# Dense expert tiles moved from the middle of the token order to its end in a streaming-encoder layer

## The chip, the core and the metric

The kernel runs on one core of one Trainium2 chip. The metric is the device time of one execution in microseconds. The core has TensorE (PE, matrix products), VectorE (DVE, elementwise work and reductions), ScalarE (ACT), GpSimd (POOL) and SyncE (SP); each takes its instructions strictly in the order in which the program lists them. SP and POOL issue DMA transfers between DRAM and the on-chip memory.

## The reference

One layer for two request groups that share weights, 1024 prompt tokens and 64 sample tokens of width 1024. Its first half is a sum of three gated branches (an mLSTM, a spatial gating unit, a cross attention). Its second half, which the change is about, is a retrieval over 16384 experts:

```python
q = (xb @ w_pq).reshape(PEER_BLOCK, PEER_HEADS, PEER_DQ)
s1 = jnp.einsum('thd,kd->thk', q[..., :half], k_sub1)
s2 = jnp.einsum('thd,kd->thk', q[..., half:], k_sub2)
v1, i1 = lax.top_k(s1, PEER_TOPK)
v2, i2 = lax.top_k(s2, PEER_TOPK)
cand = v1[..., :, None] + v2[..., None, :]            # 16 x 16 sums
sc, pos = lax.top_k(cand, PEER_TOPK)
e = jnp.take_along_axis(cidx, pos, axis=-1)           # 8 heads x 16 experts a token
g = jax.nn.softmax(sc, axis=-1)
a = jax.nn.gelu(jnp.einsum('tkd,td->tk', u_exp[e], xb))
out = jnp.einsum('tk,tkd->td', g * a, v_exp[e])
```

So each token picks 128 of the 16384 experts (8 heads, 16 each), takes a dot product with a row of `u_exp` for each, and sums rows of `v_exp` with the weights that come out. Outputs are the two normalised results and the states and caches of the first half.

## The kernel before

**Tiles and blocks.** The tokens stand in nine tiles: 0 to 7 of 128 prompt tokens and "s" of 64 sample tokens. `BLOCKS` groups them: [0, 1], [2, 3, 4, "s"], [5, 6, 7]. The first phase runs block after block: `main_block` does the projections and the output projection on PE, `mlstm` and `side` the branches, and `retrieve` the scores against the sub-keys and, on DVE, the first top-16 of each head. `choose_tile` then does, once for each tile and almost wholly on DVE, the second top-16 over 54 candidate sums, the decoding of the expert numbers and the softmax. In the second phase PE works through all 16384 experts for the dense tiles.

**Two ways through the experts.** Tiles in `GT` gather: for each of a token's 128 experts a row of `u_exp` is fetched by an indirect DMA that POOL issues (L1018, one for 128 rows of 4 KB; the sample tile packs two picks of 64 tokens into one), and DVE takes the dot product (L1031, here called a u) into a column of `av`; later a row of `v_exp` is fetched the same way and DVE adds it, weighted, to the tile's sum (L1039, a v). With four tiles of 128 and the one of 64 this is 576 u and 576 v. The landing buffers are three for u (`BU`) and four for v (`BV`), seven for the last tile's v; a buffer comes free when its u or v has run on DVE. The u of a tile run beside the v of the tile before it.

Tiles in `DENSE` (512 tokens) are instead multiplied with all experts on PE: `hidden` computes 256 experts for 512 tokens and applies the gelu, `times_g` multiplies by a table of weights that is zero but for the chosen experts, `weigh` splits the result in a high and a low part, and `dense` multiplies by `v_exp` (L1258 to L1260). The operands are split in high and low parts, which costs three products each; the low part of every weight piece is taken on DVE (L280, `wl`).

**The table.** `dense` builds it before its own expert loop, tile by tile in the order of `CHOOSE`, in groups of four tokens: DVE writes 0/1 rows by comparing with the two key numbers (L1187) and multiplies one of them by the softmax weights (L1191), here together called the hots, 256 instructions; PE multiplies the two (L1200), ACT copies the result to `sg`, and SP stores it to `gd` in DRAM. It needs `d{t}`, the end of `choose_tile` of that tile. Only four pieces of `hidden` can run ahead of the table; the expert loop on PE starts when the whole table is in DRAM and its first part has been loaded back (`g<-gd`).

**What sets the order.** Each part is a generator; `Flow.run` takes the one that has got least far, by the numbers that the generators yield, or passes over one that waits for a signal. A list scheduler then orders each engine's instructions further when the program is built. `experts` yields 2.5 a gather in the first phase and 2.2 in the second; the hots yield 1.2 a group of four tokens. In the last block `choose_tile` of the gathering tiles 6 and 7 waits for the signal "weights", which `dense` gives after its last hots.

Of the kernel before, what the change touches and what calls it, by code (L numbers as in the profile page):

```python
# [7 lines left out]
F32 = mybir.dt.float32  # L8
F32R = mybir.dt.float32r
BF = mybir.dt.bfloat16  # L10
I32 = mybir.dt.int32
# [54 lines left out]
def tile_stream_step(ctx: ExitStack, tc: tile.TileContext, a: dict, out: dict):  # L66
    nc = tc.nc
    V, S, T, G, SP = nc.vector, nc.scalar, nc.tensor, nc.gpsimd, nc.sync


    BLOCKS = [[0, 1], [2, 3, 4, "s"], [5, 6, 7]]
    TILES = [t for b in BLOCKS for t in b]

    DENSE = [2, 3, 4, 5]
    NT = max(len(b) for b in BLOCKS)
    ND = len(DENSE)
    ROWS_OF = {t: 64 if t == "s" else 128 for t in TILES}
    TD = 128 * ND
# [5 lines left out]
    gp = pool("gp", 1)  # L84
    kp = pool("kp", 1)
# [9 lines left out]
    now = {"dp": None}  # L95
# [238 lines left out]
    fl = Flow()  # L334
    st = {}
# [504 lines left out]
    def choose_tile(b, t):  # L840

        L = ROWS_OF[t]
        v16, i16 = st["k", t]
        scv = kp.tile([128, 8, 16], F32, name="scv", bufs=1)[0:L]
        if b == len(BLOCKS) - 1 and t not in DENSE:

            yield "weights"
            V.tensor_copy(scv[0:1, 0, 0:1], st["weights"][0:1])
        pos = kp.tile([128, 8, 16], U32, name="pos", bufs=1)[0:L]
        ib = kp.tile([128, 256], BF, name="ib", bufs=1)[0:L].rearrange("p (a k) -> p a k", k=16)  # L850
        V.tensor_copy(ib.rearrange("p (s h) k -> p s h k", s=2), i16.rearrange("p (h s) k -> p s h k", s=2))
# [45 lines left out]
                    V.tensor_tensor(ef, ef, oh[:, 0], op=ALU.add)  # L897
                yield 1.7
        if t not in DENSE:
            if GT.index(t) >= 3:  # L900
                yield f"free{GT[GT.index(t) - 3]}"
            go = gp.tile([128, 128], F32, name="gg", bufs=3)
            e = gp.tile([128, 128], I32, name="e", bufs=3)

            for q in range(128 // L):
                V.scalar_tensor_tensor(e[q * L:q * L + L, 0:L], ef[:, q * 64:q * 64 + L], 128.0,
                                       ef[:, 128 + q * 64:128 + q * 64 + L], op0=ALU.mult, op1=ALU.add)
        gg = kp.tile([128, 8, 16], F32, name="ggd")[0:L]
# [19 lines left out]


    GT = [t for t in TILES if t not in DENSE]  # L930
    CHOOSE = [t for b in BLOCKS for t in sorted(b, key=lambda t: (t in DENSE) != (b is BLOCKS[-1]))]

    def out_rows(t, x, r, gfin):
        n = ROWS_OF[t]
# [4 lines left out]
    def experts():  # L939
# [14 lines left out]
        def end_u(t):  # L954
            _, av = st_u.pop(t)
            e, gg = st.pop(("e", t))
            L = ROWS_OF[t]
            av, gg = av[:, 0:L], gg[:, 0:L]
            t1 = gp.tile([128, 128], F32, name="w2", bufs=2)[:, 0:L]
            S.activation(t1, av, AF.Square, scale=GELU_C ** 0.5)  # L960
            V.scalar_tensor_tensor(t1, t1, 1.0, av, op0=ALU.add, op1=ALU.mult)
            S.activation(t1, t1, AF.Tanh, scale=GELU_S)
            V.scalar_tensor_tensor(t1, t1, 1.0, av, op0=ALU.add, op1=ALU.mult)
            V.scalar_tensor_tensor(t1, t1, 0.5, gg, op0=ALU.mult, op1=ALU.mult)
            st_v[t] = (e, t1)
            fl.signal(f"u{t}")
# [82 lines left out]
        for s_ in range(len(ops)):  # L1049
            while nxt < len(ops) and (nxt <= s_ or can_issue(ops[nxt])):  # L1050
                kind, t, j = ops[nxt]
                ready = f"e{t}"
                if kind == "u" and ready not in fl.done:
                    if nxt > s_:
                        break
                    yield ready
                issue(ops[nxt])
                nxt += 1
            consume(ops[s_])

            yield 2.5 if now["dp"] is None else 2.2

    phase1 = [main(), mlstm(), side(), retrieve()]
    for g in phase1:
# [9 lines left out]
    dp = pool("dp", 1)  # L1074
# [65 lines left out]
    def dense():  # L1140
# [16 lines left out]
        x = hp.tile([128, 2560], BF, name="hotx")  # L1157
        hots.append((x[:, 0:1024], x[:, 1024:2560]))
        hots = [[x.rearrange("p (j c t) -> p j c t", c=128, t=4) for x in h] for h in hots]
        nd1 = 0  # L1160
        for i, t in sorted(enumerate(DENSE), key=lambda x: CHOOSE.index(x[1])):
            n = ROWS_OF[t]
            yield f"d{t}"
            k_ = kp.tile([128, 3, 128], F32, name="dk", tag="k4", bufs=3)[0:n]
            SP.dma_start(k_, dkd[t])
            cs = slice(i * 128, i * 128 + n)
            p = two_banks()[:, 0, :]
            for j in range(3):
                T.transpose(p[:, j * 128:j * 128 + n], k_[:, j, :], ident[0:n, 0:n])
            S.copy(kb[:, :, cs], p.rearrange("p (s t) -> p s t", s=4)[:, 0:2, 0:n])  # L1170
            gf = kp.tile([128, 128], F32, name="gf", tag="k4", bufs=3)
            S.copy(gb[:, 0, cs], p[:, 256:256 + n])
            V.tensor_tensor(gf[:, 0:n], p[:, 256:256 + n], gb[:, 0, cs], op=ALU.subtract)
            S.copy(gb[:, 1, cs], gf[:, 0:n])
            V.tensor_tensor(gb[:, 2, cs], gf[:, 0:n], gb[:, 1, cs], op=ALU.subtract)
            V.tensor_copy(gf_[:, cs], gb[:, 2, cs])
            yield 3.0

            for t0 in range(i * 128, i * 128 + n, 32):
                sg = hp.tile([128, 32, 4, 32], F32, name="sg", bufs=2)  # L1180
                for t1 in range(0, 32, 8):
                    p = two_banks()
                    for b in range(2):
                        tb = t0 + t1 + 4 * b
                        ts = slice(tb, tb + 4)
                        eq, pr = hots[tb // 4 % len(hots)]
                        V.tensor_tensor(eq, io[:, None].to_broadcast([128, 2, 128, 4]),  # L1187
                                        kb[:, :, None, ts].to_broadcast([128, 2, 128, 4]), op=ALU.is_equal)

                        nd = 2 + b  # L1190
                        V.tensor_tensor(pr[:, 0:nd], eq[:, 0, None].to_broadcast([128, nd, 128, 4]),  # L1191
                                        gb[:, 0:nd, None, ts].to_broadcast([128, nd, 128, 4]), op=ALU.mult)
                        for j in range(nd, 3):
                            for t2 in range(4):
                                S.activation(pr[:, j, :, t2], eq[:, 0, :, t2], AF.Copy,
                                             scale=gf_[:, tb + t2:tb + t2 + 1])

                        for t2 in range(4):
                            for j in range(3):
                                T.matmul(p[:, b, t2 * 128:(t2 + 1) * 128], eq[:, 1, :, t2], pr[:, j, :, t2],  # L1200
                                         start=(j == 0), stop=(j == 2))
                        yield 1.2
                    S.copy(sg[:, :, :, t1:t1 + 8].rearrange("p g c t -> p (g c) t"),
                           p.rearrange("p b (t e) -> p e (b t)", t=4))
                    yield 0.4
                nd1 += 32
                if nd1 == TD:
                    st["weights"] = tok = kp.tile([128, 1], F32, name="tok")
                    V.tensor_copy(tok, sg[:, 0, 0, 0:1])
                    fl.signal("weights")  # L1210
                SP.dma_start(gd[:, :, t0 // 32].rearrange("g p c t -> p g (c t)"),
                             sg.rearrange("p g c t -> p g (c t)"))
        yield "ahead"
# [149 lines left out]
```

## Time and profile before

| | |
|---|---|
| median of 3 runs | 3675.89 us (3674.61 to 3696.73) |
| the profiled execution | 3700.63 us, its span 3698.9 us |
| PE busy | 3280.4 us, 89% |
| DVE busy | 3102.7 us, 84% |
| POOL busy | 1721.0 us, 47% |
| ACT busy | 1367.2 us, 37% |
| moved by DMA | 1024.78 MB, mean 277 GB/s |
| mean granted PE clock | 0.932 of full speed |

The engines work at the same time, so their shares don't add to 100%. Shares over the whole span hide that different stretches have different limits. The first phase ends on DVE at about 1912 us (the first `dxl`, L1133, the operand of the dense tiles); the hots run from 1925 to 2242 us; from 2290 us to the end PE does the dense expert loop.

### The profile page before, as it was taken

Reading aid. Unit: us, or ns where it says so; the run is one execution under the profiler, and the core shown is the slowest. Engines: PE = TensorE matmul, PEld = TensorE weight load, DVE = VectorE, ACT = ScalarE, POOL = GpSimd, SP = SyncE. Lnnn points to the kernel's source line nnn. Section 1 sums busy time; section 2 is a strip of 40 time slices with the busy share of each in tenths; the row PEclk is TensorE's granted clock in tenths of the full one; section 3 lists DMA queues with packets and bytes.
Section 4 is the critical chain, followed back from the end, with each engine's and each line's share of the span. In section 5 each row is a group of like instructions: output and inputs, shape, how many; then the busy total and the mean of one; then the engine's idle time right before and its main releaser. Section 6 shows DMA issues by size and latency. Waiting matters only on the chain.

```text
span 3698.9 us, 46231 instructions
## 1 busy us (share of the span) xinstructions
PE 3280.4 (89%) x15364; PEld 2632.8 (71%) x15364; DVE 3102.7 (84%) x6492; ACT 1367.2 (37%) x2479; POOL 1721.0 (47%) x1208
## 2 busy tenths in 40 slices
PE   8999998889996595898939765998999999999998
PEld 7787876576675473776938664876678888888886
DVE  5556797768899999899998999887798888879984
ACT  5555533423333242333415653322233333333332
POOL 1001334447765775465333475444465555446540
PEclk9999999999998697998959767999999999999999
DMA  7556477788897887898867788888899999989982
GB/s 230 148 165 188 152 245 248 254 279 321 320 367 273 272 306 252 276 334 285 302 209 220 235 269 292 312 287 276 295 376 337 337 339 337 328 282 386 356 303 85
DMA packets 447436, 1024.78 MB, mean 277 GB/s; under 512 B 32182, under 2 KB 169566, under 8 KB 443100
## 3 DMA queue, kind: packets, MB, share of 16 engines
q0 software_dynamic: 166528, 604.58, 47.0%
q1 hardware_dynamic: 276828, 413.06, 33.6%
q10 hardware_dynamic: 3840, 4.20, 0.3%
q8 instruction: 120, 1.97, 0.2%
q14 instruction: 120, 0.98, 0.1%
HBM read 968.44 MB, written 53.26 MB: 276 GB/s over the span
## 4 chain that ended last, share of the span: by engine, by line
PE 46%; DVE 20%; issue 13%; DMA 11%; POOL 8%; ACT 1%; POOLq 0%; DVEq 0%; ACTq 0%; SPq 0%
DMA gu<-in_u_exp_dram,e 7%; POOL gu L1018 5%; PE po L1260 5%; PE po L1259 5%; PE po L1258 5%; PE ph L1109 4%; PE ph L1111 4%; PE ph L1110 4%; DVE gacc L1039 4%; DVE gu L1031 4%; PE acc L312 3%; PE acc L311 3%; PE acc L313 3%; DVE wl L280 2%; DMA gv<-in_v_exp_dram,e 2%
## 5 line engine op out<-in xcount | busy, mean ns | idle before, releaser
L1018 POOL DMA_INDIRECT gv<-in_v_exp_dram,e x522 | 842.1, 1613 | 671.9 <-DVE gacc L1039 294.9
L1018 POOL DMA_INDIRECT gu<-in_u_exp_dram,e x576 | 756.8, 1314 | 774.6 <-DVE gu L1031 491.2
L277 ACT CAST wh<-wraw 128x512 fp32r<-128x512 f32 x994 | 613.0, 622 | 1347.9 <-PE ph L1110 481.5
L1031 DVE SCALAR_TENSOR_TENSOR gu<-gu,gx 128x1024 f32<-128x1024 f32 x576 | 701.6, 1220 | 195.2 <-DMA gu<-in_u_exp_dram,e 192.7
L280 DVE TENSOR_TENSOR wl<-wraw,wh 128x512 fp32r<-128x512 f32 x962 | 655.0, 686 | 228.4 <-ACT wh L277 226.2
L1039 DVE SCALAR_TENSOR_TENSOR gacc<-gv,w,gacc 128x1024 f32<-128x1024 f32 x448 | 573.1, 1279 | 33.3 <-DMA gv<-in_v_exp_dram,e 32.8
L312 PE MATMUL acc<-wl,half 128*128 128x512 f32 (+1 forms) x1152 | 474.1, 412 | 4.1 <-DVE wl L280 4.1
L313 PE MATMUL acc<-wh,half 128*128 128x512 f32 (+1 forms) x1152 | 456.2, 402 | 0.0
L1258 PE MATMUL po<-wh,W 128*128 128x512 f32 x1024 | 403.2, 399 | 32.6 <-ACT W L1228 32.6
L1111 PE MATMUL ph<-dxh,wl 128*128 128x512 f32 x1024 | 403.0, 394 | 18.5 <-DVE wl L280 18.4
L311 PE MATMUL acc<-wh,half 128*128 128x512 f32 (+1 forms) x1152 | 412.0, 410 | 6.5 <-ACT uB L470 5.1
L1259 PE MATMUL po<-wl,W 128*128 128x512 f32 x1024 | 408.7, 399 | 7.9 <-DVE wl L280 7.8
L1260 PE MATMUL po<-wh,W 128*128 128x512 f32 x1024 | 407.6, 398 | 0.6 <-DVE W L1229 0.6
L1109 PE MATMUL ph<-dxh,wh 128*128 128x512 f32 x1024 | 401.5, 392 | 1.3 <-DVE dxl L1133 1.3
L1110 PE MATMUL ph<-dxl,wh 128*128 128x512 f32 x1024 | 400.9, 391 | 0.0
L328 PE MATMUL acc<-half,wh 128*128 128x256 f32 (+2 forms) x768 | 250.2, 346 | 17.8 <-ACT wh L277 13.1
L311 PEld LDWEIGHTS acc<-wh,half 128*128 128x128 f32 (+1 forms) x1152 | 210.3, 184 | 77.8 <-issue 15.1
L312 PEld LDWEIGHTS acc<-wl,half 128*128 128x128 f32 (+1 forms) x1152 | 211.7, 184 | 71.4 <-issue 12.5
L329 PE MATMUL acc<-half,wh 128*128 128x256 f32 (+2 forms) x768 | 258.9, 342 | 0.0
L1258 PEld LDWEIGHTS po<-wh,W 128*128 128x128 f32 x1024 | 194.0, 189 | 80.3 <-issue 33.7
L313 PEld LDWEIGHTS acc<-wh,half 128*128 128x128 f32 (+1 forms) x1152 | 210.7, 184 | 54.4 <-issue 1.9
L330 PE MATMUL acc<-half,wl 128*128 128x256 f32 (+2 forms) x768 | 228.4, 343 | 15.5 <-DVE wl L280 8.5
(446 smaller groups left out, 5062.1 us busy)
## 6 DMA issues: line engine op xcount, KB each, us to landing
wraw<-in_w_in_dram SPq DMA_DIRECT2D x216, 512.0 KB
wraw<-in_v_exp_dram SPq DMA_DIRECT2D x126, 512.0 KB
wraw<-in_u_exp_t_dram SPq DMA_DIRECT2D x67, 512.0 KB
gd<-sg SPq DMA_DIRECT2D x16, 2048.0 KB
g<-gd SPq DMA_DIRECT2D x32, 1024.0 KB
wrawx<-in_u_exp_t_dram SPq DMA_DIRECT2D x61, 512.0 KB
wraw<-in_w_pq_dram SPq DMA_DIRECT2D x48, 512.0 KB
wraw<-in_w_out_dram SPq DMA_DIRECT2D x24, 512.0 KB
```

What stands on the lines that cost most here:

```text
L277: S.copy(h, t)
L280: E.tensor_tensor(l, t, h.bitcast(F32), op=ALU.subtract)
L311: T.matmul(ps[i], xh[:, cs], h, start=(k == 0), stop=False)
L312: T.matmul(ps[i], xh[:, cs], l, start=False, stop=False)
L313: T.matmul(ps[i], xl[:, cs], h, start=False, stop=(last and b is None))
L1018: G.indirect_dma_start(out=tl, out_offset=None, in_=src, in_offset=bass.IndirectOffsetOnAxis(ap=col, axis=0))
L1031: V.scalar_tensor_tensor(tl, tl, 1.0, xn, op0=ALU.mult, op1=ALU.mult, accum_out=av[:, j:j + 1])
L1039: V.scalar_tensor_tensor(x2, gt_.pop(op), st_v[t][1][:, j:j + 1], x2, op0=ALU.mult, op1=ALU.add)
L1111: T.matmul(o, l[:, cs], xh[:, k + kk, :], start=False, stop=(k + kk == KD - 1))
L1258: T.matmul(o, hi, h, start=(q == 0 and k == 0), stop=False)
L1259: T.matmul(o, hi, l, start=False, stop=False)
L1260: T.matmul(o, lo, h, start=False, stop=(q == GP - 1 and k == 1))
```

## The change

Six things: `DENSE` becomes [4, 5, 6, 7], so that tiles 0, 1, 2, 3 and "s" gather (all in the first two blocks) and three of the four dense tiles are in the last block; the wait for "weights", with the token that gave it, goes; `CHOOSE` takes gathering tiles first in every block, the last one too; the buffers of the gathering tiles' expert numbers and weights become four of each instead of three, and `w2` one instead of two; `experts` yields 3.0 in the first phase and 2.0 in the second (2.5 and 2.2); the hots yield 0.3 instead of 1.2.

```diff
--- before.py
+++ after.py
@@ -71,7 +71,7 @@
     BLOCKS = [[0, 1], [2, 3, 4, "s"], [5, 6, 7]]
     TILES = [t for b in BLOCKS for t in b]
 
-    DENSE = [2, 3, 4, 5]
+    DENSE = [4, 5, 6, 7]
     NT = max(len(b) for b in BLOCKS)
     ND = len(DENSE)
     ROWS_OF = {t: 64 if t == "s" else 128 for t in TILES}
@@ -842,10 +842,6 @@
         L = ROWS_OF[t]
         v16, i16 = st["k", t]
         scv = kp.tile([128, 8, 16], F32, name="scv", bufs=1)[0:L]
-        if b == len(BLOCKS) - 1 and t not in DENSE:
-
-            yield "weights"
-            V.tensor_copy(scv[0:1, 0, 0:1], st["weights"][0:1])
         pos = kp.tile([128, 8, 16], U32, name="pos", bufs=1)[0:L]
         ib = kp.tile([128, 256], BF, name="ib", bufs=1)[0:L].rearrange("p (a k) -> p a k", k=16)
         V.tensor_copy(ib.rearrange("p (s h) k -> p s h k", s=2), i16.rearrange("p (h s) k -> p s h k", s=2))
@@ -897,10 +893,10 @@
                     V.tensor_tensor(ef, ef, oh[:, 0], op=ALU.add)
                 yield 1.7
         if t not in DENSE:
-            if GT.index(t) >= 3:
-                yield f"free{GT[GT.index(t) - 3]}"
-            go = gp.tile([128, 128], F32, name="gg", bufs=3)
-            e = gp.tile([128, 128], I32, name="e", bufs=3)
+            if GT.index(t) >= 4:
+                yield f"free{GT[GT.index(t) - 4]}"
+            go = gp.tile([128, 128], F32, name="gg", bufs=4)
+            e = gp.tile([128, 128], I32, name="e", bufs=4)
 
             for q in range(128 // L):
                 V.scalar_tensor_tensor(e[q * L:q * L + L, 0:L], ef[:, q * 64:q * 64 + L], 128.0,
@@ -928,7 +924,7 @@
 
 
     GT = [t for t in TILES if t not in DENSE]
-    CHOOSE = [t for b in BLOCKS for t in sorted(b, key=lambda t: (t in DENSE) != (b is BLOCKS[-1]))]
+    CHOOSE = [t for b in BLOCKS for t in sorted(b, key=lambda t: t in DENSE)]
 
     def out_rows(t, x, r, gfin):
         n = ROWS_OF[t]
@@ -956,7 +952,7 @@
             e, gg = st.pop(("e", t))
             L = ROWS_OF[t]
             av, gg = av[:, 0:L], gg[:, 0:L]
-            t1 = gp.tile([128, 128], F32, name="w2", bufs=2)[:, 0:L]
+            t1 = gp.tile([128, 128], F32, name="w2", bufs=1)[:, 0:L]
             S.activation(t1, av, AF.Square, scale=GELU_C ** 0.5)
             V.scalar_tensor_tensor(t1, t1, 1.0, av, op0=ALU.add, op1=ALU.mult)
             S.activation(t1, t1, AF.Tanh, scale=GELU_S)
@@ -1058,7 +1054,7 @@
                 nxt += 1
             consume(ops[s_])
 
-            yield 2.5 if now["dp"] is None else 2.2
+            yield 3.0 if now["dp"] is None else 2.0
 
     phase1 = [main(), mlstm(), side(), retrieve()]
     for g in phase1:
@@ -1157,7 +1153,6 @@
         x = hp.tile([128, 2560], BF, name="hotx")
         hots.append((x[:, 0:1024], x[:, 1024:2560]))
         hots = [[x.rearrange("p (j c t) -> p j c t", c=128, t=4) for x in h] for h in hots]
-        nd1 = 0
         for i, t in sorted(enumerate(DENSE), key=lambda x: CHOOSE.index(x[1])):
             n = ROWS_OF[t]
             yield f"d{t}"
@@ -1199,15 +1194,10 @@
                             for j in range(3):
                                 T.matmul(p[:, b, t2 * 128:(t2 + 1) * 128], eq[:, 1, :, t2], pr[:, j, :, t2],
                                          start=(j == 0), stop=(j == 2))
-                        yield 1.2
+                        yield 0.3
                     S.copy(sg[:, :, :, t1:t1 + 8].rearrange("p g c t -> p (g c) t"),
                            p.rearrange("p b (t e) -> p e (b t)", t=4))
                     yield 0.4
-                nd1 += 32
-                if nd1 == TD:
-                    st["weights"] = tok = kp.tile([128, 1], F32, name="tok")
-                    V.tensor_copy(tok, sg[:, 0, 0, 0:1])
-                    fl.signal("weights")
                 SP.dma_start(gd[:, :, t0 // 32].rearrange("g p c t -> p g (c t)"),
                              sg.rearrange("p g c t -> p g (c t)"))
         yield "ahead"
```

On DVE, near the end of the first phase (around the 560th of the 1088 `wl`; L1039 before and L1035 after are the v, L1027 is the u after), before the change:

```order
L1039 SCALAR_TENSOR_TENSOR gacc<-gv,w_17058,gacc 128x1024
L280 TENSOR_TENSOR wl<-wraw,wh 128x512
L892 TENSOR_TENSOR oh<-oh 128x512
L194 TENSOR_TENSOR rn<-rn 128x3
L280 TENSOR_TENSOR wl<-wraw,wh 128x512
L1039 SCALAR_TENSOR_TENSOR gacc<-gv,w_17058,gacc 128x1024
L896 TENSOR_TENSOR oh<-oh 128x256
L889 SCALAR_TENSOR_TENSOR oh<-xy,ib 128x256 x2
```

and of the change, at the same place:

```order
L1027 SCALAR_TENSOR_TENSOR gu,av<-gu,gx 128x1024
L1035 SCALAR_TENSOR_TENSOR gacc<-gv,w_16080,gacc 128x1024
L195 TENSOR_TENSOR rn<-rn 128x3
L280 TENSOR_TENSOR wl<-wraw,wh 128x512 x2
L1035 SCALAR_TENSOR_TENSOR gacc<-gv,w_16080,gacc 128x1024
L197 SCALAR_TENSOR_TENSOR rn<-rn 128x3
L1027 SCALAR_TENSOR_TENSOR gu,av<-gu,gx 128x1024 x2
```

Before, no u is left there, since the next gathering tile (6) is not chosen yet; after, u of tile 2 or 3 stand there beside the v, and the choosing of a dense tile (`oh`) has moved back.

On DVE, in the middle of the hots (L1187 and L1191 before, L1182 and L1186 after; `hot`, `one` and `hotx` are their rows, `oh` and `ei` belong to `choose_tile`), before the change:

```order
L1191 TENSOR_TENSOR one<-one 128x1536
L1191 TENSOR_TENSOR hotx<-hotx,one 128x1536
L1039 SCALAR_TENSOR_TENSOR gacc<-gv,w_21390,gacc 128x1024
L1187 TENSOR_TENSOR hot<-one 128x1024
L1039 SCALAR_TENSOR_TENSOR gacc<-gv,w_21390,gacc 128x1024
L1187 TENSOR_TENSOR one<-one 128x1024
L1191 TENSOR_TENSOR hot<-hot,one 128x1024
L1187 TENSOR_TENSOR one<-one 128x1024
L1039 SCALAR_TENSOR_TENSOR gacc<-gv,w_21390,gacc 128x1024
L1187 TENSOR_TENSOR hotx<-one 128x1024
L1191 TENSOR_TENSOR one<-one 128x1536
```

and of the change, during the choosing of tile 7:

```order
L1186 TENSOR_TENSOR hot<-hot,one 128x1024
L1186 TENSOR_TENSOR one<-one 128x1536
L1027 SCALAR_TENSOR_TENSOR gu,av<-gu,gx 128x1024
L1035 SCALAR_TENSOR_TENSOR gacc<-gv,w_22386,gacc 128x1024
L1186 TENSOR_TENSOR one<-one 128x1024
L1186 TENSOR_TENSOR hotx<-hotx,one 128x1536
L885 SCALAR_TENSOR_TENSOR oh<-xy,ib 128x256 x2
L1182 TENSOR_TENSOR hot<-one 128x1024
L1027 SCALAR_TENSOR_TENSOR gu,av<-gu,gx 128x1024
L1182 TENSOR_TENSOR one<-one 128x1024
L1035 SCALAR_TENSOR_TENSOR gacc<-gv,w_22386,gacc 128x1024
```

Before, only v of tiles 1 and "s" stand between the hots; after, u and v both, and the instructions that choose a later dense tile. Counted over the whole order: from the first `dxl` to the last of the 256 hots there stand 74 v and no u before, 122 v and 174 u after; the choosing there is 115 instructions before and 363 after.

On DVE, in the dense loop at the 660th of the 1088 `wl` (L1093 and L1089 are `times_g`, L1229 and L1219 `weigh`), before the change:

```order
L1031 SCALAR_TENSOR_TENSOR gu,av<-gu,gx 128x1024
L280 TENSOR_TENSOR wl<-wraw,wh 128x512
L1093 TENSOR_TENSOR ge<-ge,g_20380 128x1024
L1031 SCALAR_TENSOR_TENSOR gu,av<-gu,gx 128x1024 x2
L280 TENSOR_TENSOR wl<-wrawx,wh 128x512
L1229 TENSOR_TENSOR W<-ge,W 128x1024
L1031 SCALAR_TENSOR_TENSOR gu,av<-gu,gx 128x1024
```

and of the change:

```order
L1035 SCALAR_TENSOR_TENSOR gacc<-gv,w_26527,gacc 128x1024
L280 TENSOR_TENSOR wl<-wraw,wh 128x512
L1089 TENSOR_TENSOR ge<-ge,g_20015 128x1024
L1035 SCALAR_TENSOR_TENSOR gacc<-gv,w_26527,gacc 128x1024
L280 TENSOR_TENSOR wl<-wrawx,wh 128x512
L1035 SCALAR_TENSOR_TENSOR gacc<-gv,w_26527,gacc 128x1024 x2
L1219 TENSOR_TENSOR W<-ge,W 128x1024
```

Behind the last hots there are 256 u and 275 v before and 6 u and 237 v after; the last v stands at the 1061st `wl` before and at the 800th after.

## Rows read from the trace of the kernel before

**Rows 1.** Busy time by stretch: start:end, length, then each engine's us and count

```profile
core 0: us, PE busy (x) PEld busy (x) DVE busy (x) ACT busy (x) POOL busy (x), PEclk, DMA share, GB/s
1600.00:1912.00 312.00, 246.01 (x1164) 205.43 (x1163) 309.28 (x892) 104.76 (x202) 144.06 (x107) 0.88 0.85 284
1912.00:2242.00 330.00, 252.42 (x1792) 225.30 (x1793) 313.57 (x587) 179.93 (x367) 179.48 (x75) 0.78 0.77 240
2242.00:2290.00 48.00, 14.81 (x59) 11.47 (x58) 40.29 (x113) 10.55 (x12) 19.71 (x14) 0.61 0.84 290
...
2400.00:2700.00 300.00, 274.62 (x1137) 214.37 (x1136) 228.88 (x355) 81.05 (x121) 128.04 (x107) 0.98 0.85 290
2700.00:3300.00 600.00, 600.00 (x2604) 489.14 (x2603) 523.94 (x678) 186.82 (x273) 311.71 (x246) 1.00 0.95 338
```

**Rows 2.** DVE's groups by line and tile, 1912 to 2242 us: busy, mean ns | idle before

```profile
L1039 DVE SCALAR_TENSOR_TENSOR gacc<-gv,w,gacc 128x1024 f32<-128x1024 f32 x74 | 95.4, 1290 | 5.8 <-DMA gv<-in_v_exp_dram,e 5.8
L1191 DVE TENSOR_TENSOR one<-one 128x1536 bf16<-128x1536 bf16 (+1 forms) x64 | 52.1, 828 | 0.0
L1187 DVE TENSOR_TENSOR one<-one 128x1024 bf16<-128x1024 bf16 x64 | 44.2, 697 | 3.9 <-PE po L1200 3.9
L1191 DVE TENSOR_TENSOR hotx<-hotx,one 128x1536 bf16<-128x1536 bf16 x32 | 30.8, 963 | 0.0
L1191 DVE TENSOR_TENSOR hot<-hot,one 128x1024 bf16<-128x1024 bf16 x32 | 22.3, 696 | 0.0
L1187 DVE TENSOR_TENSOR hotx<-one 128x1024 bf16<-128x1024 bf16 x32 | 22.2, 695 | 0.7 <-PE po L1200 0.7
L1187 DVE TENSOR_TENSOR hot<-one 128x1024 bf16<-128x1024 bf16 x32 | 22.2, 694 | 3.1 <-PE po L1200 3.1
```

**Rows 3.** PE's waits from 1912 to 2300 us: total, times, longest

```profile
PE po L1258 <- ACT W L1228: 32.6, 1, 32.6
PE po L1200 <- DVE hot L1191: 26.1, 10, 7.8
PE po L1200 <- DVE one L1191: 25.4, 24, 5.4
```

**Rows 4.** DVE's groups over the whole span, shapes apart

```profile
L1031 DVE SCALAR_TENSOR_TENSOR gu<-gu,gx 128x1024 f32<-128x1024 f32 x576 | 701.6, 1220 | 195.2 <-DMA gu<-in_u_exp_dram,e 192.7 <-DMA gx<-xn2d 1.4
L1039 DVE SCALAR_TENSOR_TENSOR gacc<-gv,w,gacc 128x1024 f32<-128x1024 f32 x448 | 573.1, 1279 | 33.3 <-DMA gv<-in_v_exp_dram,e 32.8
L889 DVE SCALAR_TENSOR_TENSOR oh<-xy,ib 128x256 bf16<-128x256 bf16 x128 | 49.1, 422 | 0.1
L803 DVE FIND_INDEX8 pos<-scv,tk 128x8 uint32<-128x54 f32 x64 | 12.6, 208 | 0.0
L896 DVE TENSOR_TENSOR oh<-oh 128x256 bf16<-128x256 bf16 x24 | 6.9, 289 | 0.1
```

**Rows 5.** DVE in order of time within the hots: start, us, what

```profile
2106.99 1.27 DVE L1039 SCALAR_TENSOR_TENSOR gacc<-gv,w,gacc 128x1024 f32<-128x1024 f32 x1
2108.19 0.22 DVE L1176 CAST hot<-one 128x128 f32<-128x128 bf16 x1
2108.32 0.95 DVE L1191 TENSOR_TENSOR one<-one 128x1536 bf16<-128x1536 bf16 x1
2109.19 0.95 DVE L1191 TENSOR_TENSOR hotx<-hotx,one 128x1536 bf16<-128x1536 bf16 x1
2110.06 1.28 DVE L1039 SCALAR_TENSOR_TENSOR gacc<-gv,w,gacc 128x1024 f32<-128x1024 f32 x1
```

**Rows 6.** POOL's gathers from 1912 to 2242 us

```profile
L1018 POOL DMA_INDIRECT gv<-in_v_exp_dram,e x75 | 181.0, 2413 | 153.2 <-DVE gacc L1039 69.0 <-DVE gacc L935 30.2 <-DVE tk L801 12.3
```

**Rows 7.** POOL's gathers from 2400 to 2700 us

```profile
L1018 POOL DMA_INDIRECT gu<-in_u_exp_dram,e x104 | 124.8, 1200 | 170.4 <-DVE gu L1031 166.1 <-DVE oh L896 2.5 <-issue 1.8
L1018 POOL DMA_INDIRECT gv<-in_v_exp_dram,e x3 | 3.5, 1169 | 2.9 <-DVE gacc L1039 2.6 <-issue 0.3
```

**Rows 8.** DVE's waits from 2290 to 2700 us

```profile
DVE gu L1031 <- DMA gu<-in_u_exp_dram,e: 75.2, 49, 5.3
```

**Rows 9.** PE's waits from 2290 us to the end

```profile
PE ph L1111 <- DVE wl L280: 18.4, 16, 2.7
PE po L1259 <- DVE wl L280: 7.8, 9, 2.2
```

## Prediction

> **What bounds the kernel now.** The busy shares of the whole span (PE 89%, DVE 84%) don't say which stretch a change touches, so I read the busy times by stretch first [rows 1]. From 2290 us to the end PE does the dense loop and is the limit: in 2700 to 3300 us it is busy all of the time, 2604 products in 600 us, 0.2304 us each. In the two stretches ahead of it PE has slack, 246 of 312 us and 252 of 330 us at a granted clock of 0.88 and 0.78, and DVE has none: 309.28 of 312 us, then 313.57 of 330 us. Next I read what DVE does between the end of the first phase (1912) and the last of the hots (2242) [rows 2]: the hots, 74 v, little else, and next to no idle time ahead of any of them. Then who waits for whom [rows 3]: PE stands 32.6 us in one piece for the first weighted operand, which needs the table back from DRAM, and before that in many pieces for the hots. So DVE's queue from 1912 to 2242 us sets when the dense loop starts, and after a round trip of 48 us PE sets the rest. Whatever is put into DVE's queue ahead of the last hots delays the end; whatever is taken out of it behind them saves only what PE waits for there.
>
> **What the change moves.** By the order of the instructions, not by the constants that the generators yield (those are weighed under the rivals):
>
> Until the first `dxl`, DVE has 396 u and 217 v where it had 320 and 227, and 510 instructions of choosing where it had 585. Prices: 1.220 us a u and 1.279 us a v [rows 4]. One choosing of a full tile is some 95 instructions, among them 16 of 0.422 us and eight each of five kinds near 0.2 us, the rest between 0.2 and 0.3 us [rows 4]; my estimate from these rows is 25 us a tile, 0.27 us each. So 76 x 1.22 - 10 x 1.28 - 75 x 0.27 = 92.7 - 12.8 - 20.3 = +59.6 us of durations.
>
> From the first `dxl` to the last hots, DVE has 174 u where it had none and 122 v where it had 74, because tiles 2, 3 and "s" still gather and no signal holds them back; and the choosing of tiles 5, 6 and 7 and part of tile 4 instead of that of 5 and part of 6, 363 instructions instead of 115. So 174 x 1.22 + 48 x 1.28 + 248 x 0.27 = 212.3 + 61.4 + 67.0 = +340.7 us. The hots themselves stay 256.
>
> Durations are not time on the queue: an instruction starts about 0.08 us before the one ahead has ended. The rows show it [rows 5]: the v of 1.27 us at 2106.99 is followed at 2108.19, 1.20 us later; 0.95 us becomes 0.87. All durations from 1912 to 2242 us add to 355 us (the seven groups shown make 289.2 of it [rows 2]), in a stretch of 330 us that DVE fills. I scale by 330 / 355 = 0.93. Then the first phase ends 0.93 x 59.6 = 55 us later, since DVE is 99% busy there [rows 1], and the stretch up to the last hots grows by 0.93 x 340.7 = 317 us, from 330 to 647 us.
>
> **Can the gathers keep up with that?** That stretch now holds 296 of them. Of these 83 stand ahead of the first hots and 213 between the hots. A gather takes POOL 2413 ns beside the hots [rows 6] and 1200 ns in 2400 to 2700 us, without hots [rows 7]. 83 x 1.20 + 213 x 2.41 = 613 us of POOL, just under the 647 of DVE. Nothing less than DVE's own 647 is possible, so that is the lower end. The upper end comes from the buffers. In 2400 to 2700 us only u run, 104 in 300 us, 8.65 us for a round of three buffers, and DVE waits for them [rows 7, 8]. Among hots the own issue of a u takes 1.2 us longer and that of a v beside it can lie ahead of it, 2.4 us more: 12.25 us a round, 174 u in 713 us. The rows are nearer to the lower end, since DVE waited only 5.8 us for its v in the stretch before [rows 2], but there were no u then, which have a buffer less. I take half, 680 us: +350.
>
> What the Trainium skill says of this (SBUF — State Buffer, Who interferes with whom) speaks against the 2413 ns: a tensor_tensor on VectorE has no two-port mode and is not expected to hold up the writing of descriptors, only GpSimd's reads. The hots are all such instructions, and the trace shows a gather twice as long beside them. By the page POOL would need 296 x 1.2 = 355 us and the stretch would stay at the 647; by the row it comes close to the limit. The row decides, and the sum above holds without the page.
>
> **Behind the last hots** DVE loses 250 u and 38 v. What PE can gain is what it waits for: 18.4 + 7.8 = 26.2 us for `wl` [rows 9], which stand in DVE's queue behind u that wait 75.2 us for their data [rows 8]; they fall in 2400 to 2700 us, where PE is busy 274.6 of 300 us [rows 1]. The 237 v that remain have four buffers, and later seven, so most of that wait should go. I take -25 us, with 0 and -40 as ends (the latter if the clock, 0.98 there, comes back to 1.00 too). The round trip through DRAM stays, and so do all 5952 products of the loop, 5952 x 0.2304 = 1371 us: nothing hides DVE's lost work, for DVE becomes idle beside a PE that is full already.
>
> The other edits cost nothing. The fourth pair of buffers for expert numbers lets a tile be chosen earlier, with the effect counted above; the single `w2` is written once a tile and read by a tile's v, and a wait for it would be a few us once a tile.
>
> **The sum.** 3698.9 + 55 + 350 - 25 = 4078.9 us of span; 1.7 us lie around it in the profiled execution (3700.63), 4080.6. That execution is 24.7 us above the median of the runs; less this, 4056 us, +10%.
>
> **Rivals.**
>
> *The gathers become the limit* (chance 0.22). POOL and the u's three buffers, not DVE, set the stretch: 713 us as above, up to 800 if landings get slower too, middle 755: +75, 4131 us. For it: every gather between the hots shares POOL with slowed ones. Against: 613 us of POOL still fit in 647.
>
> *The gathers are never waited for* (0.17). Hots that stand twice as far apart no longer slow POOL; the stretch is DVE's 647: 33 us less, 4023 us. For it: a gather of 1.2 us elsewhere. Against: u have three buffers only. The page named above gives this one.
>
> *DVE's extra work is hidden* (0.04). If PE's own chain through the hots, at a clock of 0.78, set the stretch of 330 us, u and v would fill DVE's gaps and only the 55 and the -25 would be left: 3706 us, within 1%. It decides if DVE has at least 317 us of gaps there; the rows show 330 - 314 = 16 [rows 1]. The constants in the generators speak for it: 64 groups of eight tokens at 1.0 instead of 2.8, a gather each 2.0, would put 32 gathers between the hots, not 213. Against it is the order itself, which the engine can't leave.
>
> *The change doesn't do what it says*: that the gathers start without a break and without "weights" is in the order, and I see no way that it fails.
>
> **Chances.** Forecast 0.50; gathers the limit 0.22; never waited for 0.17; hidden 0.04; left over 0.07, of which 0.02 faster, 0.01 no change and 0.04 slower outside the range. About 1% is what a measurement of this kernel can tell from no change. Slower by over 1%: 0.50 + 0.22 + 0.17 + 0.04 = 0.93; within 1%: 0.05; faster: 0.02. The range goes from the low ends, first phase +30 and stretch 630 (a queue a little tighter than 0.93) and dense loop -40, 3966 us, to the high ends, +75 and 750 and 0, 4171 us; 3965 to 4170.
>
> **What the changed kernel's profile would show.** Right, if the first `dxl` comes near 1967 us with DVE over 95% busy in the 300 us ahead of it; if the last hots end 650 to 710 us later, PE under half busy at a low clock meanwhile and DVE over 90%; if gathers there take POOL about 2.4 us; and if the dense loop then takes about 1380 us at a full PE, with DVE nearly free of u and v in its second half. Wrong, if the last hots come within 400 us of the first `dxl` (the order does not bind as I think), if DVE shows long waits for u there (gathers the limit), or if the dense loop gets shorter by more than 40 us (PE was not its limit).

## The result, and the profile after

The change makes the kernel slower: 4094.45 us against 3681.89 us, medians of 4 runs each (one more run of before than in the table ahead, hence its other median), a ratio of 1.1115 (95% interval 1.1076 to 1.1154). The profiled execution of the changed kernel took 4094.61 us, its span is 4092.8 us, 393.9 us longer than that of before.

The busy times by stretch of the changed kernel, cut at its own first `dxl` (2021 us) and last hots (2665 us), answer to [rows 1]; columns are start:end, length, then each engine's busy time and count of instructions, PE's granted clock, DMA share and GB/s:

```profile
core 0: us, PE busy (x) PEld busy (x) DVE busy (x) ACT busy (x) POOL busy (x), PEclk, DMA share, GB/s
1600.00:2021.00 421.00, 274.19 (x1226) 222.54 (x1224) 380.11 (x962) 109.26 (x208) 285.72 (x180) 0.81 0.87 303
2021.00:2665.00 644.00, 262.66 (x1800) 226.13 (x1801) 623.42 (x1294) 182.80 (x372) 409.48 (x296) 0.59 0.92 306
2665.00:2714.00 49.00, 6.79 (x26) 5.07 (x26) 27.08 (x30) 5.63 (x6) 22.17 (x18) 0.51 0.89 328
...
3300.00:3900.00 600.00, 600.00 (x2605) 489.46 (x2604) 246.38 (x299) 185.51 (x271) 0.00 (x0) 1.00 0.38 120
```

Between the first `dxl` and the last hots DVE is busy for 623 of 644 us, while PE does the same 1800 or so products as before [rows 1, second stretch] and idles for 381 us, at a clock of 0.59. From 3300 to 3900 us DVE is busy for 41% and POOL not at all: the gathers have left the place where they cost next to nothing (the first experiment prices them). The span's growth splits as follows.

| from | to | before | after | difference |
|---|---|---|---|---|
| start | first `dxl` | 1912 | 2021 | +109 |
| first `dxl` | last hots | 330 | 644 | +314 |
| last hots | end of the span | 1457 | 1428 | -29 |

In that middle stretch the u, which are new there, and the v, which have become more, head DVE's list (line and tile, count, busy, mean ns, idle time before them), where [rows 2] had only 74 v and the hots:

```profile
L1027 DVE SCALAR_TENSOR_TENSOR gu<-gu,gx 128x1024 f32<-128x1024 f32 x174 | 210.6, 1212 | 16.8 <-DMA gu<-in_u_exp_dram,e 16.6
L1035 DVE SCALAR_TENSOR_TENSOR gacc<-gv,w,gacc 128x1024 f32<-128x1024 f32 x122 | 155.3, 1273 | 0.0
```

They take 366 us there, and DVE waits only 16.6 us for their data. POOL's gathers in the same stretch answer to [rows 6]:

```profile
L1014 POOL DMA_INDIRECT gu<-in_u_exp_dram,e x175 | 220.3, 1259 | 138.5 <-DVE gu L1027 85.0 <-issue 22.6 <-DVE one L1170 5.2
L1014 POOL DMA_INDIRECT gv<-in_v_exp_dram,e x121 | 190.9, 1578 | 96.3 <-DVE gacc L1035 49.9 <-issue 13.1 <-DVE scv L802 7.1
```

PE's waits in that stretch and up to the dense loop are for the hots, and now also for `dk`, the transposed choices of the next dense tile (total, times, longest):

```profile
PE po L1164 <- DMA dk<-dkd: 137.7, 4, 69.7
PE po L1195 <- DVE hot L1186: 130.3, 27, 10.3
PE po L1195 <- DVE one L1186: 53.2, 39, 4.4
```

and of PE's waits in the dense loop [rows 9] almost nothing is left:

```profile
PE ph L1107 <- DVE wl L280: 2.1, 3, 1.1
PE po L1248 <- DVE ob L1259: 0.2, 1, 0.2
```

### The profile page after: what moved, and what is told of

Same layout as the page of the kernel before. It is cut to its first block, busy times and chain, and to the rows that moved or that the text cites. A ratio compares the mean times of both kernels' runs of the same rounds, so it can differ in the third digit from the quotient of the medians.

```text
span 4092.8 us, 46192 instructions
## 1 busy us (share of the span) xinstructions
PE 3297.9 (81%) x15364; PEld 2644.3 (65%) x15364; DVE 3123.1 (76%) x6489; ACT 1365.0 (33%) x2475; POOL 1684.3 (41%) x1208
## 4 chain that ended last, share of the span: by engine, by line
PE 42%; DVE 27%; DMA 18%; issue 9%; POOL 3%; ACT 1%; DVEq 0%; SPq 0%; POOLq 0%; ACTq 0%
DMA gu<-in_u_exp_dram,e 9%; DVE gu L1027 7%; DVE gacc L1035 6%; DMA gv<-in_v_exp_dram,e 5%; PE po L1250 4%; PE po L1248 4%; PE po L1249 4%; PE ph L1107 4%; PE ph L1105 4%; PE ph L1106 4%; PE acc L311 3%; PE acc L312 3%; PE acc L313 3%; DVE wl L280 2%; POOL gu L1014 2%
## 5 line engine op out<-in xcount | busy, mean ns | idle before, releaser
L1014 POOL DMA_INDIRECT gu<-in_u_exp_dram,e x576 | 784.5, 1362 | 627.4 <-DVE gu L1027 345.5
L1014 POOL DMA_INDIRECT gv<-in_v_exp_dram,e x549 | 807.7, 1471 | 561.3 <-DVE gacc L1035 330.0
L1027 DVE SCALAR_TENSOR_TENSOR gu<-gu,gx 128x1024 f32<-128x1024 f32 x576 | 698.2, 1214 | 172.3 <-DMA gu<-in_u_exp_dram,e 169.6
L1035 DVE SCALAR_TENSOR_TENSOR gacc<-gv,w,gacc 128x1024 f32<-128x1024 f32 x512 | 653.1, 1276 | 54.2 <-DMA gv<-in_v_exp_dram,e 51.7
L313 PE MATMUL acc<-wh,half 128*128 128x512 f32 (+1 forms) x1152 | 460.3, 405 | 0.0
L311 PE MATMUL acc<-wh,half 128*128 128x512 f32 (+1 forms) x1152 | 419.1, 415 | 5.2 <-ACT uB L470 3.9
```

The costliest lines, as they stand in the source:

```text
L311: T.matmul(ps[i], xh[:, cs], h, start=(k == 0), stop=False)
L313: T.matmul(ps[i], xl[:, cs], h, start=False, stop=(last and b is None))
L1014: G.indirect_dma_start(out=tl, out_offset=None, in_=src, in_offset=bass.IndirectOffsetOnAxis(ap=col, axis=0))
L1027: V.scalar_tensor_tensor(tl, tl, 1.0, xn, op0=ALU.mult, op1=ALU.mult, accum_out=av[:, j:j + 1])
L1035: V.scalar_tensor_tensor(x2, gt_.pop(op), st_v[t][1][:, j:j + 1], x2, op0=ALU.mult, op1=ALU.add)
```

## Experiments

Three questions stood behind them: is it DVE's count of instructions ahead of the last hots that sets the delay, or the chain of choosing three tiles one after the other; which part of the change carries it; and why did the first phase end 109 us later where I had 55. "The stretch" below is always that from the first `dxl` to the last hots. Each ratio is to executions of the kernel before that were taken beside the run; their medians were 3685 to 3691 us.

### Hold the gathers of the changed kernel behind the hots

```diff
+                if nh == TD:
+                    st["hots"] = kp.tile([128, 1], F32, name="htok")
+                    V.tensor_copy(st["hots"], sg[:, 0, 0, 0:1])
+                    fl.signal("hots")
...
+            if HOLD <= nxt < HOLD + BU + BV:
+                V.tensor_copy(tl[:, 0:1], st["hots"])
             G.indirect_dma_start(out=tl, out_offset=None, in_=src,
...
+                if nxt >= HOLD and "hots" not in fl.done:
+                    if nxt > s_:
+                        break
+                    yield "hots"
```

I did not expect the signal alone to hold anything, because the list scheduler moves what is ready (no run has the signal without the token); the token written into the landing buffer is a dependency that it must respect. HOLD is 613 here. The lines marked ... are left out.

> The changed kernel, with all gathers from the 613th on held behind the last hots by a data dependency (their landing buffer is first written from a token of the hots). From the first dxl to the last hots 24 v remain instead of 122 v and 174 u; the dense loop then holds 205 u and 334 v. Theory (u and v of DVE lengthen that stretch): the stretch falls from 644 us by 0.93 x (174 x 1.22 + 98 x 1.28) = 314 us to about 330 us, the first phase ends some 35 us earlier with 25 fewer u ahead of it, the dense loop stays limited by PE (0 to +20 us): 3740 to 3770 us. Rival (the chain of choosing tiles 5, 6 and 7 one after the other, for which PE waited 137.7 us, sets the stretch): it stays over 450 us and the time over 3880 us. Second rival (the dense loop pays for the 302 gathers it gets): the loop, 1379 us from its first to its end, grows by more than 60 us.

Measured: 3722.65 us, ratio to before 1.0102 (1.0078 to 1.0127). The busy times of the stretch:

```profile
1975.00:2294.00 319.00, 253.20 (x1786) 225.14 (x1787) 303.91 (x830) 181.19 (x368) 24.06 (x22) 0.79 0.52 159
```

It fell from 644 to 319 us, with all of the choosing of tiles 5, 6 and 7 still in it, and PE's wait for `dk` fell with it:

```profile
PE po L1172 <- DMA dk<-dkd: 19.6, 3, 11.7
```

So the 137.7 us of the changed kernel were not the latency of choosing; they were the u and v that stood between its instructions. The dense loop took the 302 gathers for nothing, 1367 us from its first weighted product to its last (1369 in the changed kernel), and the whole is 372 us faster than the changed kernel. That is 17 us under my lower end; I had left 0 to 20 us for the loop.

### Hold them earlier

The same with HOLD at 547.

> The changed kernel with the gathers held from the 547th on, so that 338 u and 209 v stand ahead of the first dxl (396 and 217 in the changed kernel, 320 and 227 before) and none between it and the last hots. Theory for the first phase (it ended 108 us later, 62 us of it more DVE work and the rest waits of DVE for u): with 58 u fewer its end moves from 2021 us to 1915 to 1945 us. Rival (the other choosing order, not the u, delays the first phase): it stays over 1990 us. The stretch up to the last hots is then about 300 us, and the dense loop has 605 gathers: 3640 to 3720 us, over this if they don't fit.

Measured: 3697.3 us, ratio 1.0029 (1.0011 to 1.0048). The first `dxl` stands at 1921 us, in the range expected, so that u and v of the first phase, not the other order of choosing, made it late: 58 u and 8 v fewer, with the same choosing ahead of it, are 81 us of durations, 75 at a scale of 0.93, and it moved by 100 us. DVE still waits for u in the last 260 us ahead of it, 18.7 us against 30.4 from 1660 us on in the changed kernel:

```profile
DVE gu L1030 <- DMA gu<-in_u_exp_dram,e: 18.7, 10, 4.5
```

The stretch took 283 us. The 605 gathers behind it no longer fit quite: the last product ended at 3634 us, the last v at 3681.

### The kernel before with the dense tiles last, and nothing else

```diff
-    DENSE = [2, 3, 4, 5]
+    DENSE = [4, 5, 6, 7]
```

> The kernel before with DENSE = [4, 5, 6, 7] alone (the wait for the dense weights then concerns no tile; three pairs of buffers, the old yields). Its order has 376 u and 220 v up to the first dxl, and 200 u, 159 v and 461 instructions of choosing from there to the last hots, against 0, 74 and 114 before. Theory (DVE's count sets the stretch): it grows from 330 us by 0.93 x (200 x 1.22 + 85 x 1.28 + 347 x 0.27) = 415 us to about 745 us, the dense loop stays at PE's 1370 us: 4060 to 4130 us, so that the place of the dense tiles alone carries the whole loss. Rival (the yields or the fourth pair of buffers are needed for the loss): under 3950 us.

Measured: 4146.96 us, ratio 1.1245 (1.1209 to 1.1281), so this one line is enough for the whole loss; with the rest of the change the time is some 50 us shorter. The stretch:

```profile
1953.00:2730.00 777.00, 263.19 (x1800) 227.05 (x1801) 722.65 (x1512) 186.57 (x376) 531.07 (x360) 0.57 0.89 298
```

777 us against 745 expected: DVE is busy for 93% of it, against 97% in the changed kernel, because it waits longer for u, 47.6 us instead of 16.6:

```profile
DVE gu L1031 <- DMA gu<-in_u_exp_dram,e: 47.6, 33, 4.7
```

### The changed kernel with the dense tiles in the middle again

```diff
-    DENSE = [4, 5, 6, 7]
+    DENSE = [2, 3, 4, 5]
```

> The changed kernel with DENSE back at [2, 3, 4, 5], everything else of the change kept (no wait for the dense weights, gathering tiles chosen first in the last block, four pairs of buffers, the new yields). Up to the first dxl DVE's order has the counts of before; from there to the last hots it has 99 u and 93 v and 287 instructions of choosing, against 0, 74 and 114 before. Theory: the stretch grows by 0.93 x (99 x 1.22 + 19 x 1.28 + 173 x 0.27) = 178 us to about 507 us, the dense loop gets 10 to 30 us shorter: 3820 to 3860 us, so that the missing wait alone costs some 160 us. Rival (only the place of the dense tiles matters, the wait does nothing): 3660 to 3700 us, as before.

Measured: 3836.66 us, ratio 1.0412 (1.0377 to 1.0446), 152 us over the before of its comparison. The stretch:

```profile
1915.00:2421.00 506.00, 257.73 (x1800) 226.58 (x1801) 489.44 (x1020) 184.66 (x374) 272.64 (x194) 0.62 0.84 282
```

Up to the first `dxl` it has before's counts and before's time. Then the gathering tiles 6 and 7, chosen first and held by nothing, put 99 u among the hots. So choosing the gathering tiles of the last block last, behind the wait for "weights", is the fence that kept u out of that stretch, and it is worth some 150 us with the dense tiles in the middle. This run drops the wait together with the order of choosing, and keeps the fourth pair of buffers; no run takes the wait out alone. Nor do the parts add up: with the dense tiles last the wait concerns no tile, so the line of the run before already removes the fence.

### The new yields alone

```diff
-                        yield 1.2
+                        yield 0.3
...
-            yield 2.5 if now["dp"] is None else 2.2
+            yield 3.0 if now["dp"] is None else 2.0
```

> The kernel before with the new yields alone (3.0 and 2.0 a gather, 0.3 a group of hots). Its order on DVE has the same counts of u, v and choosing in every stretch as before, and the same order on POOL. Theory (the list scheduler, not the yields, sets the order): no change, ratio 0.995 to 1.005, 71 v between the hots still. Rival (the yields move the hots ahead of the gathers, as their numbers say, 32 gathers instead of 71): some 45 us faster, ratio under 0.99.

Measured: 3684.73 us, ratio 0.9988 (0.9973 to 1.0004): no change. The stretch took 324 us instead of 330. In the trace DVE's instructions stand in the same order as before up to the last hots; behind them, from 2304 us on, some stand a few places off. So these constants, which say which work should come first, move nothing ahead of the hand-over to the dense loop.

### The kernel before with its gathers held

HOLD at 547 in the kernel before.

> The kernel before, with all gathers from the 547th on held behind the last hots by the same dependency. Between the hots 6 v remain instead of 71; the dense loop gets 605 gathers instead of 531. Theory (gathers among the hots cost their DVE time there, and little in the dense loop, where PE is the limit): the stretch from the first dxl to the last hots falls from 329 us by 0.93 x 65 x 1.28 = 77 us to about 252 us; the whole gets 40 to 80 us faster than before, ratio 0.978 to 0.989, the difference being what the dense loop pays at its end, since its last v stands behind its last weight split. Rival (the dense loop can't take more gathers): its tail grows by as much, ratio 0.995 to 1.02.

Measured: 3641.67 us, ratio 0.9879 (0.9859 to 0.9899). The stretch, and what follows PE's last product:

```profile
1904.00:2170.00 266.00, 244.20 (x1788) 225.47 (x1788) 238.14 (x511) 177.12 (x365) 7.87 (x6) 0.93 0.54 159
...
3586.00:3641.00 55.00, 0.53 (x3) 0.10 (x1) 46.98 (x63) 3.82 (x10) 24.43 (x23) 0.52 0.79 301
```

64 us come out of the stretch, a little less than the 77 us of DVE's instructions that left it, because DVE is no longer full (238 of 266 us). The dense loop got shorter too, 1376 us from its first weighted product to its last instead of 1407, though u still have three buffers: DVE waits for u 28.7 us there, where it waited 85.9 us before from the last hots on. Some of this is given back at the end, where DVE finishes v for 45 us after PE has stopped.

### Four landing buffers for u and three for v

```diff
-    BU, BV = 3, 4
+    BU, BV = 4, 3
```

In the kernel before:

> The kernel before with four landing buffers for u and three for v, nothing held. Theory (the 75.2 us that DVE waits for u from 2290 to 2700 us, and the 26.2 us that PE waits for DVE there, come from the three buffers): PE's waits there go, and 64 instead of 71 v stand between the hots: 20 to 35 us faster, ratio 0.990 to 0.995. Rival (v with three buffers wait instead, in the first phase too): within 10 us of before, or slower.

Measured: 3653.37 us, ratio 0.9909 (0.9883 to 0.9935). DVE's wait for u from 2290 to 2700 us fell to a quarter of [rows 8], and the dense loop from 1407 to 1371 us, which is the whole gain of 37 us: the stretch took 329 us although 7 v had left it.

```profile
DVE gu L1031 <- DMA gu<-in_u_exp_dram,e: 19.7, 17, 3.4
```

In the changed kernel:

> The changed kernel with four landing buffers for u and three for v. Its order has 441 u and 209 v up to the first dxl (396 and 217 in the changed kernel) and 135 u and 108 v from there to the last hots (174 and 122). Theory for the first phase (46 us of the changed kernel's 108 us delay are waits of DVE for u with three buffers): DVE's waits for u between 1660 and 2021 us, 30.4 us, go, and 45 more u come in for 45 x 1.14 = 51 us: the first dxl near 2040 us instead of 2021; the stretch to the last hots falls by 0.93 x (39 x 1.22 + 14 x 1.28) = 61 us to about 584 us: 4040 to 4070 us. Rival (the waits come from elsewhere, or v wait in their place): the first dxl at 2070 us or later.

Measured: 4083.25 us, ratio 1.1072 (1.1036 to 1.1109), a little above the expected range. The first `dxl` came at 2032 us and the stretch took 584 us, both as expected. But the dense loop grew from 1369 to 1416 us: it starts with v alone, and DVE waits for v with three buffers, from 2640 to 3400 us, as it did for u with three.

```profile
DVE gacc L1035 <- DMA gv<-in_v_exp_dram,e: 114.1, 89, 3.5
```

And DVE's waits for u in the first phase did not go with the fourth buffer, 23.7 us from 1660 to 2010 us:

```profile
DVE gu L1027 <- DMA gu<-in_u_exp_dram,e: 23.7, 12, 4.1
```

so that the three buffers explain the waits in the dense loop of before, and are not shown to explain those in the first phase.

### Both together

> The kernel before with the gathers held from the 547th on, and landing buffers of four for u and three for v instead of three and four (the same memory). With three and four buffers the PE part of the dense loop ended at 3586 us and the last v at 3632 us. Theory (in stretches of u alone DVE waits for three buffers): DVE's waits for u in the dense loop, 28.7 us, go, the gathers end earlier and the time falls by 10 to 40 us against that kernel, ratio to before 0.978 to 0.986. Rival (the order of DVE, not the buffers, sets when the last v run): the time stays within 10 us, ratio 0.985 to 0.991; or v with three buffers wait as much as u did.

Measured: 3627.44 us, ratio 0.9844 (0.9816 to 0.9871), 14 us under the same with three and four buffers; the stretch took 267 us, and DVE finished v for 37 us behind PE's last product.

With HOLD at 575:

> The kernel before with four buffers for u and three for v, and the gathers held from the 575th on instead of the 547th. 25 v stand between the hots instead of 8, and 577 gathers instead of 605 behind them. With 547 the last PE product ended at 3579 us and the last v at 3616 us. Theory (a gather among the hots costs its DVE time at once, one behind PE's last product costs about 2 us at the end): the last hots come 20 us later and the tail behind PE is 20 to 40 us shorter: within 15 us of 3627 us. Rival (the tail does not shrink, since DVE's order spreads the v to the end of the loop): 15 to 30 us slower than it.

Measured: 3617.57 us, ratio 0.9806 (0.9789 to 0.9822), the fastest kernel here. 17 v went back among the hots (25 instead of 8) and cost 14 us there (281 us), and the last v now ends at 3589 us, ahead of PE's last product at 3596 us. The change goes against this balance: what still fits behind the last hots should not stand ahead of them. Of HOLD only these two values were tried with these buffers.

## Why the prediction was right

It said 4056 us in a range of 3965 to 4170, slower; measured is 4094.

**DVE's queue up to the last hots sets when the dense loop starts.** Right, and the runs show it. Scaling by 0.93 what each kernel's order adds to or takes from before's 330 us, as the prediction did (1.22 us a u, 1.28 us a v, 0.27 us an instruction of choosing), gives:

| kernel | u, v, choosing in the stretch | by the count | measured |
|---|---|---|---|
| before | 0, 74, 114 | 330 | 330 |
| before, buffers 4 and 3 | 0, 67, 115 | 322 | 329 |
| before, held at 547 | 0, 9, 115 | 253 | 266 |
| before, held at 547, buffers 4 and 3 | 0, 10, 115 | 254 | 267 |
| before, held at 575, buffers 4 and 3 | 0, 27, 115 | 274 | 281 |
| changed, held at 547 | 0, 0, 362 | 304 | 283 |
| changed, held at 613 | 0, 24, 362 | 333 | 319 |
| changed, dense in the middle | 99, 93, 287 | 508 | 506 |
| changed, buffers 4 and 3 | 135, 108, 362 | 586 | 584 |
| changed | 174, 122, 362 | 647 | 644 |
| before, dense last | 200, 159, 461 | 745 | 777 |

Ten orders beside before's, from 266 to 777 us, eight of them within 14 us of the count. Of the two others the changed kernel held at 547 is 21 us shorter, and the kernel before with the dense tiles last 32 us longer, where DVE waits 47.6 us for u. The 0.93 itself is a little high: its 355 us add up groups, in which overlaps are already taken out, and the single durations add to 362 us, which makes 0.91 and about 640 us for the changed kernel instead of 647.

**The stall on top of it.** The prediction took 680 us, halfway between DVE's 647 and 713 from the buffers. Measured is 644: the term of 33 us was too large by all of it. Its price was the 2413 ns a gather [rows 6], carried over to hots that stand among u, v and choosing. There a gather took 1259 and 1578 ns, POOL 411 us in all and not 613, and DVE's wait for u 16.6 us. (58 rounds of 12.25 us are also 711 us and not 713; half the way is 680 all the same.) For this stretch the rival "never waited for" was the better one. The kind of stall is real, though: with the dense tiles last and nothing else changed, the stretch took the 32 us over the count that the prediction had looked for here.

**The first phase.** Predicted +55, measured +109: this is the term that failed. It took DVE as 99% busy there as it was before [rows 1], with no wait for u, and DVE is busy for 380 of 421 us up to its end. Of the difference, waits of DVE for u make 34.1 us in the stretch from 1600 us, where before there was 0.9:

```profile
DVE gu L1027 <- DMA gu<-in_u_exp_dram,e: 34.1, 19, 5.8
```

The prediction asked whether gathers could keep up in the second stretch and did not ask it for the first, where the u go on beside the last projection's weights. A further part is variation: the 508th `wl` came 19 us later than before after the same counts of u, v and choosing to within five, and in the changed kernel held at 547, whose order is the same up to there, it came 17 us earlier again. The rest, under 10 us, is open, and so is what the waits for u hang on, since a fourth buffer took away only part of them.

**The dense loop.** Predicted -25, measured -29 from the last hots to the end. The loop itself went from 1407 to 1369 us, to the 1371 that its products need, and the round trip through DRAM got some 8 us longer. PE's 26.2 us of waits went to 2.1, as said; another 14 us come from PE's products themselves, busy for 1367 us instead of 1380, at a granted clock of 1.00 instead of 0.99 over the loop. The prediction had that part only in its low end. That PE gains no more, however idle DVE becomes, is the 600.00 of 600 us above.

**The sum.** +54 in the first phase, -36 in the stretch and -4 behind it leave the span 14 us above the predicted 4079. The other 25 us are the correction from the profiled execution of before to its median, which the changed kernel does not have: its profiled execution, 4094.61 us, lies at its median. That the sum came within 1% is luck in part: the first phase was 54 us too small and the stretch 36 us too large, and the two errors mostly cancel.

**The signs.** Three of those named for a right prediction did not come: the first `dxl` stood at 2021 us and not near 1967, DVE was 92% busy in the 300 us ahead of it and not over 95%, and the gathers took 1.3 to 1.6 us and not 2.4. The stretch, at 644 us, lies just under its 650 to 710.

**The rivals.** "Hidden" fell with the stretch of 644 us. "Gathers the limit" fell with POOL's 411 us in 644. The constants of the generators, named as what spoke for a small change, move nothing ahead of the last hots by the run with the yields alone.

## What to carry to other kernels

When one engine ends each stage and another the next, count what stands in the first one's queue ahead of the hand-over, by the final order of instructions; work that is free after the hand-over costs its full time ahead of it. A wait that looks like a brake can be the fence that keeps such work behind the hand-over, so move it rather than remove it: here a fence at the right count and one buffer moved, in the kernel before, gave 0.9806 of its time; the change, which has no fence, took 1.11 of it, and the change with a fence 1.003. And don't count on a generator's constants as a fence where a scheduler reorders: here they moved nothing ahead of the hand-over, and a dependency did.

## What the runs showed of the hardware

The cost of an indirect gather on POOL beside bf16 tensor_tensor work on DVE is not one number. With v alone between runs of hots it took 2413 ns [rows 6]; with u, v and choosing between them 1259 ns (u) and 1578 ns (v). In time order, POOL and DVE alone, before the change (start, length, engine, what):

```profile
2116.41 3.21 POOL L1018 DMA_INDIRECT gv<-in_v_exp_dram,e x1 [0.66 <-DVE gacc L1039]
2116.66 1.55 DVE L1191 TENSOR_TENSOR one<-one 128x1536 bf16<-128x1536 bf16 x2
2118.13 0.69 DVE L1187 TENSOR_TENSOR hot<-one 128x1024 bf16<-128x1024 bf16 x1
2118.73 1.28 DVE L1039 SCALAR_TENSOR_TENSOR gacc<-gv,w,gacc 128x1024 f32<-128x1024 f32 x1
2119.93 0.95 DVE L1191 TENSOR_TENSOR hotx<-hotx,one 128x1536 bf16<-128x1536 bf16 x1
2120.28 2.62 POOL L1018 DMA_INDIRECT gv<-in_v_exp_dram,e x1 [0.66 <-DVE gacc L1039]
2120.79 0.69 DVE L1191 TENSOR_TENSOR hot<-hot,one 128x1024 bf16<-128x1024 bf16 x1
2121.40 0.69 DVE L1187 TENSOR_TENSOR one<-one 128x1024 bf16<-128x1024 bf16 x1
2122.00 1.28 DVE L1039 SCALAR_TENSOR_TENSOR gacc<-gv,w,gacc 128x1024 f32<-128x1024 f32 x1
```

and in the changed kernel:

```profile
2502.98 0.67 DVE L1186 TENSOR_TENSOR one<-one 128x1024 bf16<-128x1024 bf16 x1
2503.32 1.15 POOL L1014 DMA_INDIRECT gv<-in_v_exp_dram,e x1 [0.65 <-DVE gacc L1035]
2503.58 0.27 DVE L892 TENSOR_TENSOR oh<-oh 128x256 bf16<-128x256 bf16 x1
2503.78 0.74 DVE L885 SCALAR_TENSOR_TENSOR oh<-xy,ib 128x256 bf16<-128x256 bf16 x2
2504.45 1.21 DVE L1027 SCALAR_TENSOR_TENSOR gu<-gu,gx 128x1024 f32<-128x1024 f32 x1
```

Both long gathers end 0.9 us after DVE has gone from hots to a v (2119.62 after 2118.73, 2122.90 after 2122.00); the short one had one hot beside its start. But how many hots follow each other without a break doesn't explain it: this gather of the changed kernel, of a u, starts beside three hots in a row and takes 1.15 us.

```profile
2518.72 0.69 DVE L1186 TENSOR_TENSOR one<-one 128x1024 bf16<-128x1024 bf16 x1
2519.07 1.15 POOL L1014 DMA_INDIRECT gu<-in_u_exp_dram,e x1 [0.97 <-DVE gu L1027]
2519.32 0.95 DVE L1186 TENSOR_TENSOR hotx<-hotx,one 128x1536 bf16<-128x1536 bf16 x1
2520.19 0.68 DVE L1182 TENSOR_TENSOR hot<-one 128x1024 bf16<-128x1024 bf16 x1
2520.79 1.28 DVE L1035 SCALAR_TENSOR_TENSOR gacc<-gv,w,gacc 128x1024 f32<-128x1024 f32 x1
```

From the first hots on, 13 gathers of a u in the changed kernel start so, beside three or more hots, and none takes over 1.51 us; 32 gathers of a v in the kernel before start so and take 3.29 us on average. So whether a gather is of a u or a v, or something that goes with it, counts too. The Trainium skill (SBUF — State Buffer, Who interferes with whom) says that a tensor_tensor with both inputs in SBUF contends with GpSimd's reads, and infers that the writing of descriptors is not held up. The u's 1259 ns agree with the second; the 2413 ns of before don't, unless the reads of a gather are what was held up. No run here isolates the cause.
